# A ring of 16 activation chunks, more weight buffers, and two more pairs with seven products in the gated MLPs of a hybrid decoder

## The chip, the cores and the metric

The kernel runs on one NeuronCore of a Trainium2 chip. The metric is the device time of one execution in microseconds; of several runs the median is given.

## What is computed

The reference is a trunk of two decoder layers, on 256 tokens of width 2048, in float32. Layer 0 mixes by gated linear attention, layer 1 by forgetting attention; both also attend to 256 memory tokens. After each mixer stands the channel mixer, in which the changed work lies (the rotation of the weight parts is written anew for the whole kernel):

```
def conv_ffn(h, w_up, conv_w, conv_b, w_down):
    u = causal_dwconv(h @ w_up, conv_w, conv_b)      # 2048 -> 2 x 5632, width 3 along the tokens
    a, val = split_cols(u, [FFN_HIDDEN, FFN_HIDDEN])
    return (jax.nn.silu(a) * val) @ w_down           # 5632 -> 2048

h = rmsnorm(x, norm_ffn[i])
x = x + conv_ffn(h, ffn_w_up[i], ffn_conv_w[i], ffn_conv_b[i], ffn_w_down[i])
```

## The kernel before

**Float32 by parts.** Every float32 operand of a matmul is taken as a high part (a copy in the fp32r format) and a low part (the rest). A product is three matmuls: high by high, low by high, high by low. ScalarE makes the high part of a weight (`casts`, L242, for pairs L391), VectorE the low part (`lows`, L243, L392).

**Units.** The weights lie in memory in units of 128 x 1024 (512 KB). A unit is loaded by SyncE's queue into a raw slot, split, and multiplied. In the feed-forward (`pair_steps`) a unit has a contraction of 128, two blocks of 128 tokens and two blocks of 512 columns, so 2 x 2 products, 12 matmuls. Raw slots are five pieces of one tile, `home`; `raw_slot` takes the oldest. While a feed-forward runs, two more (`guests`, in the tile `raw2`) join at its first pair with sevens and leave at its end. High and low parts rotate through five tiles each (`whi`, `wlo`), everywhere in the kernel.

**Pairs with sevens.** Two units in a row can be done as a 2 x 2 block product with seven products instead of eight (21 matmuls instead of 24), if sums of the two units' activations and sums of the weights are at hand. The weights' sums are four VectorE additions in place (L448 to L451). The activations' sums are made once: for the up projection by `input_sums` (chunks 6 and, for the panels in `MORE_IN`, 11), for the down projection by `token_sums` when the chunk is made (`SEVEN_DOWN`: chunks 4, 10, 20, 34). After the last such pair of a panel, `early` reads four of its eight banks and adds them up (eight VectorE operations in the down projection); after the last unit, `late` reads the other four.

**Order of the feed-forward.** The hidden width is 44 chunks of 128. `up 0`, `up 4`, ... stand here for the projections of four chunks each (`up_pair(j)`: 16 units for both halves of the gate). The down projection goes in three panels, chunks 0 to 15, 16 to 27 and 28 to 43 (`PARTS`). After up 16 follows down panel 0, with the column blocks 0 and 1 (f=0) and then 2 and 3 (f=2), 16 units each; after up 28 down panel 1, 12 units each; after up 40 the last panel. In the panels 0 and 1, f=0 has no pairs with sevens, f=2 has those of chunks 4 and 10, or 20.

**The convolution.** A panel of four chunks leaves its projection as tokens by channels. It is turned by VectorE (`yu`, L1478) and by a round trip through DRAM on GpSimd's queue: one transfer out (`far`, L661) and four back (`fvt` or `yzu`, L666), for each half of a panel. Then come, for each half, 12 taps on ScalarE (L1428, into three tiles `taps`), two additions of 1024 columns on VectorE (L1435), a SiLU (L1441), the product (L1448, into the tile `cv`) and the split into the ring `m` (L539, L540), with the token sums of the chunks that need them. These steps are put into the program by ticks: each unit is a tick, which adds a credit (1.45, or 1.7 in panels with two pairs; none in a pair), and a step is issued when its due tick has come and credit is left. The return is issued three ticks after the panel's end, the taps come due seven or eight ticks after it. So the convolution of a panel runs beside the units of the next: that of panel 16 beside down panel 0, that of panel 28 beside down panel 1.

**The ring.** The result of the convolution, chunk c, lies in `m[c % 20]`: 16 tiles of a buffer and four more, in layer 0 in the place of the second layer's memory keys and values, which are parked in DRAM meanwhile (`more`), in layer 1 in tiles of its own.

The engines' order of instructions is worked out by a scheduler at build time, from priorities and simulated times; splits and loads have a priority ahead (`AHEAD`), and `issue_after` keeps an instruction behind another on its engine.

Of the kernel before, what the change touches and what calls it, by code (L numbers as in the profile page):

```python
# [30 lines left out]
TAU = 16.0  # L31
BIG = 1e30
PARTS = ((0, 16), (16, 28), (28, 44))
RING = 20
SEVEN_UP = (6,)
SEVEN_DOWN = {4: 0, 10: 1, 20: 0, 34: 1}
SEVEN_MORE = 11
MORE_IN = (1, 2, 5, 6, 7, 8, 9, 10)
SCRATCH = 4096
RAWS = 5  # L40


LEVELS = (64, 16, 4)
# [105 lines left out]
def _trunk(ctx: ExitStack, tc: tile.TileContext, xt, xtok, memt, wp, wgu, gns, gfin, cnv, par, msk, out):  # L149
# [38 lines left out]
    home = rear.tile([P, RAWS * NUNIT], F32, name="raw")  # L188
    slots, coming = [home[:, i * NUNIT : (i + 1) * NUNIT] for i in range(RAWS)], []

    def raw_slot():

        slots.append(slots.pop(0))
        return slots[-1]
    scratch = [sm]
    parked = []

# [5 lines left out]
    def split_apart(unit, spare):  # L203

        off, kcs, n = unit
        w = len(kcs) * n
        with tc.high_priority(offset=AHEAD):
            raw = raw_slot()
            loads.append(nc.sync.dma_start(raw[:, :w], wp[off : off + P * w].rearrange("(p n) -> p n", p=P)))
            hi, lo = [], []  # L210
            for j in range(len(kcs)):
                s = slice(j * n, (j + 1) * n)
                hi.append(spare())
                lo.append(spare())
                casts.append(S.activation(hi[j], raw[:, s], AF.Copy))
                lows.append(V.tensor_tensor(lo[j], raw[:, s], hi[j].bitcast(F32), ALU.subtract))
        return hi, lo

    def split_unit(unit, pieces=1, before=None, between=int):

        off, kcs, n = unit
        w = len(kcs) * n
        with tc.high_priority(offset=AHEAD):
            raw = raw_slot()
            hi = wpool.tile([P, NUNIT], F32R, name="whi", tag="whi", bufs=5)
            lo = wpool.tile([P, NUNIT], F32R, name="wlo", tag="wlo", bufs=5)
            src = wp[off : off + P * w].rearrange("(p n) -> p n", p=P)
            for i in range(pieces):
                s = slice(i * w // pieces, (i + 1) * w // pieces)
                if i:  # L230
                    between()
                loads.append(nc.sync.dma_start(raw[:, s], src[:, s]))
            if n % P:
                a, b, c = (t.rearrange("p (j m) -> p j m", j=len(kcs))[:, :, :n] for t in (raw[:, :w], hi, lo))
                casts.append(S.activation(b, a, AF.Copy))
                lows.append(V.tensor_tensor(c, a, b.bitcast(F32), ALU.subtract))
                return hi, lo
            for i in range(pieces):
                s = slice(i * w // pieces, (i + 1) * w // pieces)
                if before is not None:  # L240
                    before(i)
                casts.append(S.activation(hi[:, s], raw[:, s], AF.Copy))  # L242
                lows.append(V.tensor_tensor(lo[:, s], raw[:, s], hi[:, s].bitcast(F32), ALU.subtract))  # L243
        return hi, lo
# [141 lines left out]
    def split_more(src, n):  # L386

        with tc.high_priority(offset=AHEAD):
            hi = wpool.tile([P, NUNIT], F32R, name="whi", tag="whi", bufs=5)
            lo = wpool.tile([P, NUNIT], F32R, name="wlo", tag="wlo", bufs=5)  # L390
            casts.append(S.activation(hi[:, :n], src, AF.Copy))  # L391
            lows.append(V.tensor_tensor(lo[:, :n], src, hi[:, :n].bitcast(F32), ALU.subtract))  # L392
        return hi, lo

    def pair_steps(units, src, sums, flip, pool, early, late, ahead=0):
# [38 lines left out]
        for k in plan:  # L434
            if k in sums:
                with tc.high_priority(offset=AHEAD):
                    slots[:0] = coming
                    del coming[:]
                    ra, rb = raw_slot(), raw_slot()
                    with tc.issue_after(loads[-1].ins):  # L440
                        for t, (off, _, w) in ((ra, units[k]), (rb, units[k + 1])):
                            loads.append(nc.sync.dma_start(t, wp[off : off + P * w].rearrange("(p n) -> p n", p=P)))
# [39 lines left out]

    def token_sums(r, dst):

        t = r.rearrange("p s (b n) -> p (s b) n", b=2)
        a11, a21, a12, a22 = (t[:, n, :] for n in range(4))
        V.tensor_tensor(a22, a21, a22, ALU.add)
        V.tensor_tensor(a21, a11, a21, ALU.subtract)
        V.tensor_tensor(a11, a22, a11, ALU.subtract)
        V.tensor_tensor(a12, a12, a11, ALU.subtract)  # L490
        halves([dst[:, part] for part in range(2)], t)

    def run(step, hooks={}, count=8):

# [202 lines left out]
    def halves(dst, src):  # L697
        S.activation(dst[0], src, AF.Copy)
        V.tensor_tensor(dst[1], src, dst[0].bitcast(F32), ALU.subtract)
# [705 lines left out]
    def ffn(l, nx, h, m, ys, zs, landing, then, pool, temps, last=None, spare=None):  # L1405
        with tc.tile_pool(name=f"ffn{l}", bufs=1) as fp:
            def held(name, i):
                return pool.tile([P, 2, 4, P], F32R, name=name, tag=f"{name}{i}")

            up_sums = {k: held("usum", k) for k in (*SEVEN_UP, SEVEN_MORE)}  # L1410
            rooms = {i: held("dsum", i) for i in range(2)}
            guest = pool.tile([P, 2 * NUNIT], F32, name="raw2")
            guests = [guest[:, i * NUNIT : (i + 1) * NUNIT] for i in range(2)]
            coming.extend(guests)
            cw = fp.tile([P, 4 * 88], F32, name="cw")
            nc.sync.dma_start(cw, cnv[l])
            taps = [fp.tile([P, 2, 2, T + i], F32, name=f"tap{i}") for i in range(3)]
# [24 lines left out]

            def gated(j, s):

                if s == 0:
                    product[0] = fp.tile([P, 2, T], F32, name="cv", tag="cv")
                    with tc.issue_after(lows[-1].ins):
                        V.tensor_tensor(product[0], taps[0][:, :, 0, :], taps[0][:, :, 1, :], ALU.mult)  # L1448
# [8 lines left out]
            product = [None]  # L1457

            def input_sums(k):

                r = fp.tile([P, 2, T], F32, name="cv", tag="cv")
                for s in range(2):
                    V.tensor_tensor(r[:, s, :], h[k + s][:, 0, :].bitcast(F32), h[k + s][:, 1, :].bitcast(F32), ALU.add)
                token_sums(r, up_sums[k])
# [141 lines left out]
            slots[:] = [s for s in slots if not any(s is g for g in guests)]  # L1606

    def preparing(name, dst, pool, far, kept=None, tag="blk", queue=nc.sync):

# [43 lines left out]
    with tc.tile_pool(name="stash", bufs=1) as st:  # L1653
# [4 lines left out]
        with tc.tile_pool(name="turn1", bufs=1) as tp:  # L1658
# [23 lines left out]
    with tc.tile_pool(name="store", bufs=1) as op:  # L1682
# [131 lines left out]
```

## Time and profile before

| | us |
|---|---|
| runs | 2209.04, 2209.77, 2210.29 |
| median | 2209.77 |
| profiled execution, its own time | 2210.43 |
| its span, first to last instruction | 2208.6 |
| TensorE busy | 2195.5 (99%) |
| VectorE busy | 1828.1 (83%) |
| ScalarE busy | 1435.6 (65%) |
| GpSimd busy | 136.8 (6%) |
| feed-forward of layer 0, about | 457 to 1106 |
| feed-forward of layer 1, about | 1494 to the end |

The busy time of an engine counts its instructions without waiting. The ends of matmuls are modelled: a matmul of 512 columns is drawn longer (0.39 us) than its distance to the next, so starts say more than busy time does. A row of windows gives for a stretch its length and then each engine's busy time and number of instructions. In a row of the timeline, "[0.23 <-ACT whi L391]" is the idle time of the engine before the instruction and what ended it. PE is TensorE's matmul, PEld its weight load, DVE VectorE, ACT ScalarE, POOL GpSimd, SP SyncE.

### The profile page before, as it was taken

The numbers are of one execution on the slowest core, as the hardware profiler recorded it, in microseconds if no ns is written. First come the engines' busy times: TensorE is split into PE (matmuls) and PEld (weight loads), VectorE is DVE, ScalarE is ACT, GpSimd is POOL, SyncE is SP. The second block draws the span as 40 slices with busy tenths as digits, with TensorE's granted clock in tenths as the row PEclk, the third lists the DMA queues.
The fourth block names the chain that finished last, engine by engine and source line by source line (L and its number), as shares of the span: only waits on it lengthen the run. The fifth ranks groups of instructions, "written<-read, shape, count | busy, mean of one in ns | idle before, by whom it ended". The sixth has DMA issues, their size and how long they took to land.

```text
span 2208.6 us, 30197 instructions
## 1 busy us (share of the span) xinstructions
PE 2195.5 (99%) x10285; PEld 1845.1 (84%) x10285; DVE 1828.1 (83%) x2715; ACT 1435.6 (65%) x2280; POOL 136.8 (6%) x257
## 2 busy tenths in 40 slices
PE   9999999999999999999999999999999999999998
PEld 7888888888888888888888998888888888888886
DVE  7768976689998889889987669668898888988996
ACT  6655655557787468657865555555888657765874
POOL 0000000001100000001010000000100000100000
PEclk9999999999999999999999999999999999999999
DMA  9767667776777567666877767776777667776783
GB/s 371 249 223 220 194 211 228 250 237 227 245 254 253 185 226 252 221 223 222 269 244 248 227 201 245 225 242 228 233 261 230 232 200 246 244 235 210 232 282 112
DMA packets 166291, 515.41 MB, mean 233 GB/s; under 512 B 20780, under 2 KB 42552, under 8 KB 166136
## 3 DMA queue, kind: packets, MB, share of 16 engines
q1 hardware_dynamic: 149064, 460.99, 63.4%
q0 software_dynamic: 16496, 51.71, 7.4%
q8 instruction: 80, 1.31, 0.2%
q10 hardware_dynamic: 576, 0.79, 0.1%
q14 instruction: 75, 0.61, 0.1%
HBM read 469.62 MB, written 43.79 MB: 232 GB/s over the span
## 4 chain that ended last, share of the span: by engine, by line
PE 95%; DVE 2%; DMA 1%; ACT 1%; issue 0%; SPq 0%; DVEq 0%; ACTq 0%
PE acc L421 27%; PE acc L347 26%; PE ps_s L421 15%; PE ps_o L421 7%; PE ps_t L421 7%; PE acc L318 3%; PE acc L273 3%; PE ps_s L347 2%; PE acc L377 2%; PE acc L271 1%; ACT whi L391 0%; DMA raw<-wp 0%; DMA far<-blk 0%; DVE wlo L392 0%; PE ps_s L1046 0%
## 5 line engine op out<-in xcount | busy, mean ns | idle before, releaser
L243 DVE TENSOR_TENSOR wlo<-raw,whi 128x1024 fp32r<-128x1024 f32 (+2 forms) x685 | 815.3, 1205 | 211.7 <-ACT whi L242 194.6
L242 ACT ACTIVATE whi<-raw 128x1024 fp32r<-128x1024 f32 (+2 forms) x685 | 703.1, 1045 | 339.7 <-PE acc L347 137.7
L391 ACT ACTIVATE whi<-raw 128x1024 fp32r<-128x1024 f32 (+1 forms) x184 | 173.8, 954 | 180.6 <-DVE raw L449 67.8
L347 PE MATMUL acc<-whi,B 128*128 128x512 f32 (+3 forms) x1248 | 290.8, 369 | 0.0
L347 PEld LDWEIGHTS acc<-whi,B 128*128 128x128 f32 x1248 | 226.8, 188 | 28.1
L392 DVE TENSOR_TENSOR wlo<-raw,whi 128x1024 fp32r<-128x1024 f32 (+1 forms) x184 | 199.2, 1088 | 35.7 <-ACT whi L391 30.6
L421 PE MATMUL acc<-whi,mix 128*128 128x512 f32 x746 | 191.3, 389 | 0.0
L421 PE MATMUL acc<-whi,B 128*128 128x512 f32 x720 | 187.4, 389 | 0.0
L421 PEld LDWEIGHTS acc<-whi,mix 128*128 128x128 f32 x746 | 140.0, 188 | 29.2
L347 PE MATMUL acc<-wlo,B 128*128 128x512 f32 (+3 forms) x624 | 159.1, 369 | 0.0
L421 PEld LDWEIGHTS acc<-whi,B 128*128 128x128 f32 x720 | 135.1, 188 | 28.3
L347 PEld LDWEIGHTS acc<-wlo,B 128*128 128x128 f32 x624 | 114.2, 188 | 14.6
L1428 ACT ACTIVATE tap<-fvt,cw 128x256 f32<-128x256 f32 x264 | 120.4, 535 | 5.1 <-DMA fvt<-far 5.1
L1428 ACT ACTIVATE tap<-yzu,cw 128x256 f32<-128x256 f32 x264 | 120.3, 533 | 4.3 <-DMA yzu<-far 3.5
L1435 DVE TENSOR_TENSOR tap<-tap,tap 128x1024 f32<-128x1024 f32 x88 | 107.1, 1217 | 14.2 <-ACT tap L1428 13.9
L421 PE MATMUL acc<-wlo,mix 128*128 128x512 f32 x373 | 105.2, 389 | 0.0
L421 PE MATMUL acc<-wlo,B 128*128 128x512 f32 x360 | 104.0, 389 | 0.0
L421 PE MATMUL ps_s<-whi,mix 128*128 128x512 f32 x374 | 103.8, 389 | 0.0
L421 PE MATMUL ps_s<-whi,B 128*128 128x512 f32 x324 | 89.9, 389 | 0.0
L421 PEld LDWEIGHTS ps_s<-whi,mix 128*128 128x128 f32 x374 | 70.2, 188 | 14.6
L421 PEld LDWEIGHTS acc<-wlo,mix 128*128 128x128 f32 x373 | 70.0, 188 | 14.5
L421 PEld LDWEIGHTS acc<-wlo,B 128*128 128x128 f32 x360 | 67.6, 188 | 14.0
(503 smaller groups left out, 3921.4 us busy)
## 6 DMA issues: line engine op xcount, KB each, us to landing
raw<-wp SPq DMA_DIRECT2D x741, 512.0 KB, 4.6
fvt<-far POOLq DMA_DIRECT2D x100, 128.0 KB, 4.8
raw<-wp SPq DMA_DIRECT2D x32, 384.0 KB, 3.5
far<-yu POOLq DMA_DIRECT2D x22, 512.0 KB, 3.1
far<-yzu POOLq DMA_DIRECT2D x22, 512.0 KB, 3.2
yzu<-far POOLq DMA_DIRECT2D x88, 128.0 KB, 4.6
raw<-wp SPq DMA_DIRECT2D x24, 388.0 KB, 3.6
x<-xtok SPq DMA_DIRECT2D x8, 512.0 KB, 7.2
```

Source lines behind the costliest of these rows:

```text
L242: casts.append(S.activation(hi[:, s], raw[:, s], AF.Copy))
L243: lows.append(V.tensor_tensor(lo[:, s], raw[:, s], hi[:, s].bitcast(F32), ALU.subtract))
L271: mm = TE.matmul(acc[p][c][:, :T], w[:, s], both[:, 0, :], start=False, stop=end and j == 3)
L273: mm = TE.matmul(acc[p][c], w[:, s], both, start=u == j == 0, stop=end and j == 3)
L318: mm = TE.matmul(acc[b][:, :n], src[kcs[j] - base][:, part, b * P : (b + 1) * P], w, start=u == 0 and low == part == j == 0, stop=u == end ...
L347: mm = TE.matmul(acc[b][:, :n], src[kc - base][:, part, b * P : (b + 1) * P], ready[low][:, j * room : j * room + n], start=i == low == pa ...
L377: mm = TE.matmul(acc[b][:, :n], src[kc - base][:, part, b * P : (b + 1) * P], w, start=i == low == part == j == 0, stop=i == end and low = ...
L391: casts.append(S.activation(hi[:, :n], src, AF.Copy))
L392: lows.append(V.tensor_tensor(lo[:, :n], src, hi[:, :n].bitcast(F32), ALU.subtract))
L421: r = TE.matmul(bank[name], x, w, start=name not in begun, stop=last)
L1428: S.activation(by_run(taps[i][:, s, c, i:]), zs[slot][:, :, 2 * c + s], AF.Copy if i else AF.Identity, bias=0.0 if i else w[3], scale=w[2 ...
L1435: V.tensor_tensor(taps[0], taps[0], taps[n][:, :, :, :T], ALU.add)
```

## The change

- The ring has 16 tiles, those of the buffer. So chunk 16 goes to the tile of chunk 0, which down panel 0 reads.
- The convolution of panel 16 comes due 30 ticks after the panel instead of 8, that of panel 28 after 22 ticks (`PUT_OFF`).
- The two places of 128 x 1024 that the ring gives up become a sixth high and a sixth low part, for the length of a feed-forward. High, low and raw now rotate by one class, `Ring`, over slices of one tile each.
- A third raw guest, so eight raw slots in the feed-forward.
- f=0 of down panel 0 takes chunk 10, and of panel 1 chunk 20, as a pair with sevens (`ONCE`).
- The product is made in place in `taps[0]`; `cv` is gone. `input_sums` works in `temps(3)`, the fourth temporary of `early`, in the pool `turn1` or `store`.
- `SCRATCH`, the build's `dynamic_dma_scratch_size`, is 2048 instead of 4096.

```
-RING = 20
+RING = 16
-SCRATCH = 4096
-RAWS = 5
+SCRATCH = 2048
+SLOTS = 5
+RAW_GUESTS = 3
+PUT_OFF = {16: 30, 28: 22}
+ONCE = {0: 10, 1: 20}
...
+    class Ring:
+        def __init__(self, home):
+            self.slots, self.coming = [home[:, i * NUNIT : (i + 1) * NUNIT] for i in range(SLOTS)], []
+        def take(self):
+            self.slots.append(self.slots.pop(0))
+            return self.slots[-1]
+        def join(self):
+            self.slots[:0] = self.coming
+            del self.coming[:]
+        def leave(self, guests):
+            self.slots[:] = [s for s in self.slots if not any(s is g for g in guests)]
+
+    raws = Ring(rear.tile([P, SLOTS * NUNIT], F32, name="raw"))
+    his, los = [Ring(wpool.tile([P, SLOTS * NUNIT], F32R, name=name, tag=name, bufs=1)) for name in ("whi", "wlo")]
...
-            raw = raw_slot()
-            hi = wpool.tile([P, NUNIT], F32R, name="whi", tag="whi", bufs=5)
-            lo = wpool.tile([P, NUNIT], F32R, name="wlo", tag="wlo", bufs=5)
+            raw = raws.take()
+            hi, lo = his.take(), los.take()
...
-                    slots[:0] = coming
-                    del coming[:]
-                    ra, rb = raw_slot(), raw_slot()
+                    for ring in (raws, his, los):
+                        ring.join()
+                    ra, rb = raws.take(), raws.take()
...
-            guest = pool.tile([P, 2 * NUNIT], F32, name="raw2")
-            guests = [guest[:, i * NUNIT : (i + 1) * NUNIT] for i in range(2)]
-            coming.extend(guests)
+            guest = pool.tile([P, RAW_GUESTS * NUNIT], F32, name="raw2")
+            guests = [guest[:, i * NUNIT : (i + 1) * NUNIT] for i in range(RAW_GUESTS)]
+            for ring, lent in ((raws, guests), (his, more[:1]), (los, more[1:])):
+                ring.coming.extend(lent)
...
+                r = taps[0][:, :, 0, :]
                 if s == 0:
-                    product[0] = fp.tile([P, 2, T], F32, name="cv", tag="cv")
                     with tc.issue_after(lows[-1].ins):
-                        V.tensor_tensor(product[0], taps[0][:, :, 0, :], taps[0][:, :, 1, :], ALU.mult)
-                r = product[0]
+                        V.tensor_tensor(r, r, taps[0][:, :, 1, :], ALU.mult)
...
             def input_sums(k):
-                r = fp.tile([P, 2, T], F32, name="cv", tag="cv")
+                r = temps(3).rearrange("p (s t) -> p s t", s=2)
...
-                turns = [turn(j + 2 * h_, 7 if not h_ and j // 4 + 1 in MORE_IN else 8) for h_ in range(2)]
+                turns = [turn(j + 2 * h_, PUT_OFF.get(j) or (7 if not h_ and j // 4 + 1 in MORE_IN else 8)) for h_ in range(2)]
...
-                    drive(down_pair(l, p, f, src, {c - lo: t for c, t in sums.items() if f}, count[2] % 2, pool,
+                    drive(down_pair(l, p, f, src, {c - lo: t for c, t in sums.items() if f or c == ONCE[p]}, count[2] % 2, pool,
                                     lambda: (temps(0), temps(1))))
...
-                more.append(const.tile([P, 2, 2, T], F32R, name="more" + tag, tag=tag))
-            ffn(0, n, bufB, bufA + [t[:, i] for t in more for i in range(2)], ys, turned3, ys, then, tp, temps)
+                more.append(const.tile([P, NUNIT], F32R, name="more" + tag, tag=tag))
+            ffn(0, n, bufB, bufA, more, ys, turned3, ys, then, tp, temps)
...
-        more = [op.tile([P, 2, T], F32R, name=f"more{i}") for i in range(RING - KC)]
-        ffn(1, n, bufA, bufB + more, ys, zs, zs, then, op, temps, last, spare)
+        more = [op.tile([P, NUNIT], F32R, name=f"more{i}") for i in range(2)]
+        ffn(1, n, bufA, bufB, more, ys, zs, zs, then, op, temps, last, spare)
```

More of the change, by code (lines that the diff above doesn't have):

```diff
@@ L187, in _trunk @@
     loads, casts, lows, ends, last_mm, sent = [], [], [], [], [], []
[L188 to L194, printed above, removed]
+    class Ring:
[11 more added lines that the diff above has]
+    his, los = [Ring(wpool.tile([P, SLOTS * NUNIT], F32R, name=name, tag=name, bufs=1)) for name in ("whi", "wlo")]
     scratch = [sm]
@@ L223, in split_unit @@
         with tc.high_priority(offset=AHEAD):
-            raw = raw_slot()
-            hi = wpool.tile([P, NUNIT], F32R, name="whi", tag="whi", bufs=5)
-            lo = wpool.tile([P, NUNIT], F32R, name="wlo", tag="wlo", bufs=5)
+            raw = raws.take()
+            hi, lo = his.take(), los.take()
             src = wp[off : off + P * w].rearrange("(p n) -> p n", p=P)
@@ L388, in split_more @@
         with tc.high_priority(offset=AHEAD):
-            hi = wpool.tile([P, NUNIT], F32R, name="whi", tag="whi", bufs=5)
-            lo = wpool.tile([P, NUNIT], F32R, name="wlo", tag="wlo", bufs=5)
+            hi, lo = his.take(), los.take()
             casts.append(S.activation(hi[:, :n], src, AF.Copy))
@@ L483, in token_sums @@
     def token_sums(r, dst):
-        t = r.rearrange("p s (b n) -> p (s b) n", b=2)
-        a11, a21, a12, a22 = (t[:, n, :] for n in range(4))
+        t = r.rearrange("p s (b n) -> p s b n", b=2)
+        a11, a21, a12, a22 = (t[:, s, b] for s in range(2) for b in range(2))
         V.tensor_tensor(a22, a21, a22, ALU.add)
@@ L490, in token_sums @@
         V.tensor_tensor(a12, a12, a11, ALU.subtract)
-        halves([dst[:, part] for part in range(2)], t)
+        halves([dst[:, part].rearrange("p (s b) n -> p s b n", s=2) for part in range(2)], t)
     def run(step, hooks={}, count=8):
@@ L1403, in add_out, with ffn @@
                 proj_tm((*key, f), src, last if f == 3 and last is not None else evac_of(f), spare if f == 3 else None)
-    def ffn(l, nx, h, m, ys, zs, landing, then, pool, temps, last=None, spare=None):
+    def ffn(l, nx, h, m, more, ys, zs, landing, then, pool, temps, last=None, spare=None):
         with tc.tile_pool(name=f"ffn{l}", bufs=1) as fp:
@@ L1455, in gated @@
                         token_sums(r, sums[j])
-            product = [None]
             def input_sums(k):
-                r = fp.tile([P, 2, T], F32, name="cv", tag="cv")
+                r = temps(3).rearrange("p (s t) -> p s t", s=2)
                 for s in range(2):
@@ L1605, in ffn @@
                         hooks.get((f, u), int)()
-            slots[:] = [s for s in slots if not any(s is g for g in guests)]
+            for ring, lent in ((raws, guests), (his, more[:1]), (los, more[1:])):
+                ring.leave(lent)
     def preparing(name, dst, pool, far, kept=None, tag="blk", queue=nc.sync):
```

## The prediction

> **What bounds the kernel now.** I read the page's busy times first, then the chain that ended last, then who TensorE waited for, and then the feed-forward stages one by one.
>
> ```profile
> span 2208.6 us, 30197 instructions
> PE 2195.5 (99%) x10285; PEld 1845.1 (84%) x10285; DVE 1828.1 (83%) x2715; ACT 1435.6 (65%) x2280; POOL 136.8 (6%) x257
> PE 95%; DVE 2%; DMA 1%; ACT 1%; issue 0%; SPq 0%; DVEq 0%; ACTq 0%
> ...
> 883.82 32.64 PE acc L421 x144
> ...
> PE ps_t L421 <- ACT whi L391: 2.0, 4, 1.2
> ```
>
> TensorE is busy for 99% of the span and carries 95% of the chain. The chain row gives its beat: 144 matmuls of 512 columns in 32.64 us, 0.2267 us per matmul with no hole. The last row lists most of what it waited for in the feed-forward pairs: 2.0 us for ScalarE's high part of a summed weight (L391). So the time is a count of matmuls times 0.2267 us, plus small stalls, as long as ScalarE and VectorE prepare weights faster than one unit per 12 matmuls, 2.72 us.
>
> ```profile
> core 0: us, PE busy (x) PEld busy (x) DVE busy (x) ACT busy (x) POOL busy (x), PEclk, DMA share, GB/s
> ...
> 501.10:543.30 42.20, 42.20 (x188) 34.95 (x187) 37.80 (x44) 32.93 (x51) 5.45 (x10) 1.00 0.71 233
> 543.30:585.50 42.20, 41.90 (x184) 33.91 (x183) 39.51 (x49) 32.73 (x52) 5.46 (x10) 1.00 0.71 236
> ...
> 671.20:714.70 43.50, 43.50 (x194) 36.02 (x193) 36.67 (x42) 31.52 (x52) 5.47 (x10) 1.00 0.78 255
> 714.70:756.80 42.10, 42.10 (x187) 34.88 (x186) 36.20 (x44) 21.38 (x23) 0.00 (x0) 1.00 0.60 199
> 756.80:799.10 42.30, 42.30 (x188) 35.02 (x187) 33.06 (x37) 23.08 (x26) 0.00 (x0) 1.00 0.60 201
> ...
> 841.20:883.80 42.60, 42.54 (x188) 34.92 (x187) 42.17 (x55) 34.30 (x57) 5.51 (x10) 1.00 0.75 241
> ...
> 1986.00:2028.20 42.20, 42.20 (x188) 34.95 (x187) 33.44 (x37) 22.98 (x26) 0.00 (x0) 1.00 0.63 207
> ...
> 457.00:1106.00 649.00, 648.35 (x2855) 535.10 (x2854) 575.69 (x713) 453.01 (x678) 60.32 (x110) 1.00 0.71 235
> 1494.00:2143.00 649.00, 647.42 (x2851) 534.36 (x2850) 575.25 (x712) 454.48 (x679) 60.40 (x110) 1.00 0.71 236
> ```
>
> These are, of the first layer, up 4, up 8, the first two column blocks of down panel 0 (f=0), its other two (f=2), up 20 and up 28, and up 32 of the second; the last two rows are all of each layer's feed-forward. TensorE idles 0.65 + 1.58 = 2.23 us in 1298 us. Its clock is 1.00 throughout. VectorE is the second engine: 42.17 of 42.60 us in up 28 and 39.51 in up 8, the stages where a convolution meets two pairs with sevens; up 20 and up 32 have two pairs too, but no convolution, and VectorE has 9 us free.
>
> **The pairs (SEVEN and ONCE).** A unit costs 12 matmuls, so a plain pair 24; a pair with sevens costs 7 products of 3, 21. The change makes one pair of f=0 in down panel 0 (chunk 10) and one in down panel 1 (chunk 20) such a pair, in both layers: 4 x 3 = 12 matmuls fewer, 12 x 0.2267 = 2.72 us, all on the path. The Trainium skill ("TensorE: Matmul & The Clock Gate", Back-to-back issue gap) puts a warm 512-column matmul at 215.7 ns start to start; by it the sum would be 2.59 us, and the trace's rows read 5% more. The row decides.
>
> What a pair adds elsewhere is read from these rows.
>
> ```profile
> L243 DVE TENSOR_TENSOR wlo<-raw,whi 128x1024 fp32r<-128x1024 f32 x196 | 235.4, 1221 | 37.5 <-ACT whi L242 35.6
> L392 DVE TENSOR_TENSOR wlo<-raw,whi 128x512 fp32r<-128x512 f32 x23 | 15.9, 689 | 11.3 <-ACT whi L391 8.7 <-PE acc L421 2.5
> L448 DVE TENSOR_TENSOR raw<-raw 128x512 f32<-128x512 f32 x23 | 15.9, 690 | 0.3
> L1435 DVE TENSOR_TENSOR tap<-tap,tap 128x1024 f32<-128x1024 f32 x41 | 49.9, 1216 | 8.9 <-ACT tap L1428 8.7
> L1448 DVE TENSOR_TENSOR cv<-tap 128x512 f32<-128x512 f32 x20 | 13.7, 685 | 0.0
> L540 DVE TENSOR_TENSOR mix<-cv,mix 128x256 fp32r<-128x256 f32 x24 | 9.2, 421 | 0.0
> L1428 ACT ACTIVATE tap<-fvt,cw 128x256 f32<-128x256 f32 x252 | 114.8, 535 | 5.1 <-DMA fvt<-far 5.1
> ```
>
> VectorE splits 0.69 + 3 x 1.22 us and forms four sums of 0.69, 7.1 us against 2 x 1.22; f=0 now also runs the early read-out, eight operations of 0.69 (5.5 us, the size of the sums' row). Together +10.2 us per pair, beside TensorE. In down panel 0 f=0 VectorE had 36.67 of 43.50 us. The convolution of panel 16 leaves it: four adds of 1.22, two products of 0.69, four splits of 0.42 are 7.9 us; nearly all of them lay there. So about 36.7 - 7 + 10.2 = 39.9 of 42.8 us. Hidden; if the cover fails, one pair costs what a pair in up 8 costs (0.51 us, below). The raw loads, two of 512 KB, stay two. ScalarE's casts grow by 1.5 units a pair, in a stage where it had 31.5 of 43.5 us.
>
> **The ring of 16 and the put-off.** Panels 16 to 19 now write over m[0..3], which down panel 0 still reads, so their convolution comes due 30 ticks after their projection instead of 8, three ticks before up 20 begins. Of the 48 taps, adds and splits of both halves a few taps stay ahead of up 20, the rest falls into up 20: VectorE 33.06 + 7.9 = 41.0 of 42.2 us, ScalarE 23.08 + 24 taps of 0.535 + some 3 = 39 at most. The same for panel 28 and up 32: 33.44 + 7.9 = 41.3. Both stand below up 28's 42.17, which stalls little. The POOL queue's two round trips (far, four returns) are issued when they were; only the readers are later, so the slot of the return stays taken longer, until the middle of up 20; the next returns are not due before its end. Cost from both sides: no stall, or the worst that such a stage shows now:
>
> ```profile
> 555.24 1.07 PE L421 MATMUL ps_s<-whi,usum 128*128 128x512 f32 x4
> 556.38 0.74 PE L421 MATMUL ps_t<-whi,usum 128*128 128x512 f32 x2
> ...
> 568.80 0.85 PE L421 MATMUL ps_s<-whi,usum 128*128 128x512 f32 x3
> 569.88 0.74 PE L421 MATMUL ps_t<-whi,usum 128*128 128x512 f32 x2 [0.23 <-ACT whi L391]
> ...
> 559.08 4.29 ACT L1428 ACTIVATE tap<-fvt,cw 128x256 f32<-128x256 f32 x10
> 563.26 0.63 ACT L391 ACTIVATE whi<-raw 128x512 fp32r<-128x512 f32 x1
> ...
> 567.32 1.06 ACT L391 ACTIVATE whi<-raw 128x1024 fp32r<-128x1024 f32 x1 [1.98 <-DVE raw L449]
> 568.77 1.06 ACT L391 ACTIVATE whi<-raw 128x1024 fp32r<-128x1024 f32 x1 [0.39 <-PE acc L421]
> ```
>
> Three matmuls from 568.80 on the beat end at 569.48; the next starts at 569.88 and the one after it 0.34 later: 0.40 + 0.11 = 0.51 us, of which the profile shows 0.23 as idle. Up 8's other pair, four matmuls from 555.24 and the next at 556.38 instead of 556.15, loses 0.23 + 0.11 by the same reckoning, so a bad stage costs 0.85. Four stages: 0 to 3.4 us; I take 0.3 each, nearer to up 28, which shows 0.06 of idle at one place, than to up 8: 1.2 us.
>
> **Sixth high and low part.** In those rows ten taps stand ahead of the pair's first cast, and its last cast waits for a part that TensorE still holds. One more part lets the casts be queued one unit, 2.72 us, sooner, five times the stall. Eleven places in both layers stall, 2.23 us of shown idle plus about 0.28 each that the modelled ends hide: 5.3 us. The first pair of each layer is another matter (next part, 2.0 us), and one at the end of layer 1 is not a pair (0.6). So 0 to 2.7 us can be gained here; I take 1.2, and it cancels the put-off. In layer 0 the two guests lie where mk1 and mv1 were parked at the very start, so they are free at once.
>
> **Eighth raw slot.**
>
> ```profile
> raw<-wp SPq DMA_DIRECT2D x741, 512.0 KB, 4.6
> ...
> fvt<-far POOLq DMA_DIRECT2D x100, 128.0 KB, 4.8
> ```
>
> A load lands in 4.6 us, and seven slots already hold seven units of 2.72 us; the eighth gains nothing, and loads that start sooner only wait longer: 0.
>
> **First pair of a layer.**
>
> ```profile
> 1498.01 5.31 DMA far<-blk
> ...
> 1503.71 5.30 DMA raw<-wp
> ...
> 1503.41 0.63 ACT L698 ACTIVATE usum<-cv 128x512 fp32r<-128x512 f32 x1 [1.45 <-DMA far<-blk]
> 1504.80 0.43 DVE L1463 TENSOR_TENSOR cv<-mix 128x256 f32<-128x256 f32 x1
> L488 DVE TENSOR_TENSOR cv<-cv 128x128 f32<-128x128 f32 x5 | 1.5, 296 | 0.0
> ...
> 1514.07 0.73 PE L421 MATMUL ps_t<-whi,usum 128*128 128x512 f32 x2 [1.18 <-ACT whi L391]
> ```
>
> The guests' loads start when far<-blk has landed, land 5.30 us later, and the fourth cast comes late: 1.18 us shown. Three guests in one tile wait the same way, so this stays. What moves: the input sums of unit 6 now use temps(3), in the pool whose usum waits for that landing too (the third row). Two adds of 0.43, four sums of 0.30, ScalarE's half 0.63 and VectorE's, 0.69 like the sums above, make 3.4 us after 1503.3: 1506.7, while the pair's loads land at 1509. Nothing, up to 3.4 us per layer if they are queued badly. The sums of unit 11 have to wait until panel 0's fourth temp is read, so 2.7 us of VectorE move to up 4 (37.80 to 40.5): 0, at most another 0.9. The product in place frees cv, and taps[0] must wait for two splits (0.8 us) more; eight taps of the other two tiles (3.4 us and more) come first: 0.
>
> **SCRATCH at half.** It is the memory that the build sets aside for POOL's transfers. No row shows how much of it they use; the nearest is this.
>
> ```profile
> 603.00 2.18 POOL L666 DMA_DIRECT2D fvt<-far  x4 [4.44 <-ACT whi L391]
> ```
>
> A burst of four takes 0.55 us each, without a pause, once ScalarE has freed the slot. I take 0. From below nothing is gained; from above see the last rival.
>
> **Sum.** -2.72 + 1.2 - 1.2 = -2.7 us. The profiled execution took 2210.43 us, its span 2208.6; it stands 0.66 above the median 2209.77. Span 2205.9, profiled time 2207.7, median 2207.0. A measurement tells 0.2% (4.4 us) from no change at best, so this is "no change" by that measure.
>
> **Rivals.** A, the sixth part clears the stalls and the put-off adds none: -2.72 - 2.7 = -5.4, 2204.4. For it: ten taps ahead of a cast. Against: in up 28 the lack is VectorE time, not parts. B, up 20 and up 32 stall as up 8 does and nothing clears: -2.72 + 3.4 = +0.7, 2210.5; the change then gives back what it saves. For it: 41.0 of 42.2 us. C, VectorE becomes the bound of up 20 and up 32: its idle in those stages (9 us) is waiting for casts and cannot all be used; if 5 us cannot, it needs 46 us of 42.2, 3.8 us lost in each of four stages: -2.7 + 15.2, 2222. It decides from 1.8 us per stage. Against: up 28 fills 42.17 of 42.60. D, POOL's transfers are held up. The Trainium skill ("SBUF — State Buffer", Summary: rules for kernel authors) says GpSimd's descriptor writing starves while VectorE has the shared port in its fast modes; the rows show bursts of 2.18 us beside a full VectorE, so it does not show today. As a mechanism here: if each return waited for the landing of the one before, a burst would take 4 x 4.8 = 19 us and a panel's two end 34 us late; 6 us are spare (four ticks of 2.72 less a landing) and six prepared units give 16, so some 12 us per panel and, over 22 panels, 2470.
>
> **How the numbers follow.** Forecast (2205.4 to 2209) 0.58, A (2203.5 to 2205.4) 0.12, B (2209 to 2211.5) 0.20, C 0.08, D 0.02. Predicted 2207.0. The range takes the forecast and about three quarters of A and of B, 0.82 in all: 2204.0 to 2211.0; C and D stay out. Faster by over 0.2% (under 2205.35) is A, 0.12; slower is C and D, 0.10; the rest, 0.78, is within.
>
> **What would show it.** Right: f=0 of down panel 0 42.8 us long (43.5 now) and of panel 1 32.0 (32.6), three matmuls fewer each; no convolution before the last units of f=2; up 20 with VectorE near 41 us and TensorE idle under 0.3; up 8 with less than its 0.30 idle. Wrong: a first pair waiting longer than 1.18 us, TensorE waiting for L391 in up 20 or up 32 by more than 1 us each, a POOL burst longer than 2.2 us, or holes in the other layers' stages, where five parts stay five.

## The result and the profile after

The changed kernel takes 2223.58 us (median of four runs, 2220.95 to 2225.07); the kernel before, beside it on the same chip, 2209.40 (2209.04 to 2210.29). The ratio is 1.0062, 95% interval 1.0045 to 1.0080: slower by 14 us, where 2207.0 was forecast and 2211.0 was the end of the range. The page of the profiled execution (its own time 2225.07):

```profile
span 2223.3 us, 30061 instructions
PE 2198.0 (99%) x10273; PEld 1840.9 (83%) x10273; DVE 1853.4 (83%) x2771; ACT 1440.0 (65%) x2292; POOL 136.7 (6%) x257
PE 92%; DVE 3%; ACT 2%; DMA 2%; issue 1%; POOL 0%; DVEq 0%; ACTq 0%; POOLq 0%
```

TensorE has 12 matmuls fewer, as counted in the forecast, and is still 14.7 us later at the end. VectorE is at 83% as before. GpSimd's 136.7 us are the 136.8 of before, with half the scratch memory. The chain has lost 3% to VectorE, ScalarE and DMA. Whom TensorE waited for (us in total, times, longest):

```profile
PE ps_t L434 <- ACT whi L404: 3.9, 2, 2.0
PE acc L434 <- ACT whi L404: 3.4, 5, 1.7
PE acc L434 <- DVE wlo L257: 2.3, 4, 1.4
PE acc L434 <- ACT whi L256: 1.8, 3, 0.7
```

L404 and L256 are the casts of the pairs and of the single units (L391 and L242 before), L257 the single units' low part. Waits for a cast are longer, and waits for low parts and for single units are new in the feed-forward. By stages of layer 0, in windows (length, busy time of each engine, clock):

```profile
core 0: us, PE busy (x) PEld busy (x) DVE busy (x) ACT busy (x) POOL busy (x), PEclk, DMA share, GB/s
669.65:712.50 42.85, 42.85 (x191) 35.48 (x190) 37.45 (x48) 20.91 (x25) 5.47 (x10) 1.00 0.74 247
...
754.65:799.40 44.75, 42.79 (x187) 34.67 (x186) 37.00 (x46) 27.37 (x40) 0.00 (x0) 1.00 0.52 180
799.40:843.60 44.20, 42.84 (x188) 34.71 (x187) 38.90 (x46) 31.54 (x48) 5.52 (x10) 1.00 0.75 241
843.60:885.75 42.15, 42.15 (x187) 34.90 (x186) 40.26 (x54) 30.47 (x45) 5.49 (x10) 1.00 0.73 257
949.70:1083.00 133.30, 128.71 (x559) 103.91 (x558) 118.95 (x146) 91.07 (x135) 10.96 (x20) 1.00 0.67 228
```

These are down panel 0 f=0, up 20, up 24, up 28, and up 32 to up 40 together. The first is what the pair promised, 42.85 us without a hole. Up 20 idles 1.96 us and up 24 1.36; up 24 has no convolution of the put-off kind. VectorE has 37.00 of 44.75 us in up 20: it is not full. Up 28, the fullest stage before, has no hole. Up 32 to up 40 idle 4.6 us; none of these three lost over 0.3 us before.

A count of the same kind for every kernel of this document: of the distances between two matmul starts, whatever goes beyond 0.2267 us (of those over 0.24), added up over both layers' feed-forward. It is taken from one profiled execution of each kernel; that of "the change, in order" was the slowest of its 11 runs, 3.6 us above their median. The column of casts is explained below, the kernels under the experiments.

| us | casts out of order | first pairs (up 0) | up 8 | up 12, 16 | up 20, 24 | down panel 1 | up 28 to 40 | all, with the rest |
|---|---|---|---|---|---|---|---|---|
| before | 4 | 2.0 | 1.8 | 0 | 0 | 0 | 1.2 | 6.1 |
| the change | 119 | 0.2 | 0.5 | 0 | 7.5 | 0 | 11.7 | 22.9 |
| pairs alone | 4 | 0.9 | 1.7 | 0 | 0 | 1.9 | 1.2 | 7.0 |
| put-off alone | 4 | 2.8 | 1.7 | 0 | 0 | 0 | 0 | 6.3 |
| the change, no pairs | 103 | 1.2 | 1.3 | 0 | 5.9 | 0 | 7.8 | 16.2 |
| the change, cv back | 135 | 0 | 0.4 | 10.0 | 5.0 | 6.8 | 25.0 | 49.5 |
| fixed slices alone | 84 | 0 | 7.2 | 7.5 | 0 | 1.8 | 2.9 | 23.6 |
| the change, free tiles | 5 | 1.9 | 3.0 | 0 | 0 | 0.4 | 0 | 7.2 |
| pairs and put-off | 4 | 1.2 | 1.7 | 0 | 0 | 1.4 | 0 | 6.1 |
| product in place alone | 4 | 3.7 | 3.0 | 0 | 0 | 0 | 0 | 8.5 |
| fixed slices, in order | 6 | 3.5 | 0.1 | 0 | 0 | 0 | 0 | 5.4 |
| the change, in order | 7 | 5.7 | 2.3 | 0 | 0 | 0 | 0 | 11.8 |
| the change, cv back, in order | 5 | 1.2 | 0.7 | 0 | 0 | 3.1 | 3.7 | 8.6 |
| pairs and put-off, fixed slices, in order | 6 | 2.1 | 0.1 | 0 | 0 | 1.4 | 2.2 | 7.6 |

22.9 - 6.1 - 2.72 for the matmuls saved = 14.1 of the span's 14.7 us: the time lies in the feed-forwards, in holes of TensorE.

What such a hole looks like, in up 20 (timeline; ScalarE, VectorE, TensorE one after the other):

```profile
769.75 1.57 ACT L404 ACTIVATE whi<-raw 128x512 fp32r<-128x512 f32 x2
771.22 1.05 ACT L404 ACTIVATE moremk<-raw 128x1024 fp32r<-128x1024 f32 x1
779.30 1.06 ACT L256 ACTIVATE whi<-raw 128x1024 fp32r<-128x1024 f32 x1 [7.02 <-PE ps_s L434]
780.27 1.04 ACT L256 ACTIVATE moremk<-raw 128x1024 fp32r<-128x1024 f32 x1
781.21 1.04 ACT L404 ACTIVATE whi<-raw 128x1024 fp32r<-128x1024 f32 x1
782.16 1.05 ACT L256 ACTIVATE whi<-raw 128x1024 fp32r<-128x1024 f32 x1
...
777.12 0.69 DVE L463 TENSOR_TENSOR raw<-raw 128x512 f32<-128x512 f32 x1
780.39 1.23 DVE L257 TENSOR_TENSOR wlo<-raw,whi 128x1024 fp32r<-128x1024 f32 x1 [2.58 <-ACT whi L256]
781.54 0.68 DVE L464 TENSOR_TENSOR raw<-raw 128x512 f32<-128x512 f32 x1
...
779.36 0.62 PE L434 MATMUL ps_s<-whi,B 128*128 128x512 f32 x2
780.26 0.39 PE L434 MATMUL ps_s<-moremv,usum 128*128 128x512 f32 x1
782.31 1.20 PE L434 MATMUL acc<-whi,usum 128*128 128x512 f32 x4 [1.65 <-ACT whi L404]
```

Which unit a row belongs to comes from matching the built program with the trace, instruction by instruction. The casts at 779.30 and 780.27 are those of units 13 and 14 of the panel. The one at 781.21 is a cast of the pair 11 and 12, which the program has two units earlier, and TensorE waits for it from 780.5 to 782.31. Its sum of weights (L463) was there at 777.8. But ScalarE runs its instructions in their order (in the trace they come line by line as in the built list): unit 13's cast stands ahead of it and waited 7.02 us for matmuls into the bank ps_s; unit 14's follows, 1.9 us for both. Unit 13's slice is, in the built program, the one in which the pair's own first high part lay, so its cast had to wait until the pair's matmuls had read that part. Units 9 and 10, which the program also has ahead of 13, are cast only after that (782.16 and later). On VectorE the same: the pair's last sum (L464) stands behind unit 13's low part, which waited 2.58 us. A cast or low part of a later unit thus holds up an earlier one.

This inversion can be counted in the built programs, on ScalarE's list of some 910 weight casts: before, 4 stand behind one that the program has later; after, 119. The table's column has this count for every kernel: the four kernels with 84 to 135 have holes of 16 to 50 us, the ten with 4 to 7 have 5.4 to 11.8.

### The profile page after: what moved, and what is told of

The parts are those of the page before. It is cut to its first block, busy times and chain, and to the rows that moved or that the text cites. A ratio compares the mean times of both kernels' runs of the same rounds, so it can differ in the third digit from the quotient of the medians.

```text
span 2223.3 us, 30061 instructions
## 1 busy us (share of the span) xinstructions
PE 2198.0 (99%) x10273; PEld 1840.9 (83%) x10273; DVE 1853.4 (83%) x2771; ACT 1440.0 (65%) x2292; POOL 136.7 (6%) x257
## 4 chain that ended last, share of the span: by engine, by line
PE 92%; DVE 3%; ACT 2%; DMA 2%; issue 1%; POOL 0%; DVEq 0%; ACTq 0%; POOLq 0%
PE acc L361 26%; PE acc L434 26%; PE ps_s L434 14%; PE ps_o L434 7%; PE ps_t L434 6%; PE acc L332 3%; PE acc L287 3%; PE ps_s L361 2%; PE acc L391 2%; PE acc L285 1%; DMA raw<-wp 1%; ACT whi L256 1%; DVE wlo L257 1%; DVE wlo L405 1%; ACT tap L1442 1%
## 5 line engine op out<-in xcount | busy, mean ns | idle before, releaser
L257 DVE TENSOR_TENSOR wlo<-raw,whi 128x1024 fp32r<-128x1024 f32 (+2 forms) x610 | 725.6, 1198 | 198.3 <-ACT whi L256 181.0
L256 ACT ACTIVATE whi<-raw 128x1024 fp32r<-128x1024 f32 (+2 forms) x610 | 629.6, 1043 | 402.9 <-PE acc L361 141.6
L361 PEld LDWEIGHTS acc<-whi,B 128*128 128x128 f32 x1248 | 226.8, 188 | 28.1
L405 DVE TENSOR_TENSOR wlo<-raw,whi 128x1024 fp32r<-128x1024 f32 (+1 forms) x164 | 176.5, 1084 | 35.9 <-ACT whi L404 22.9
L404 ACT ACTIVATE whi<-raw 128x1024 fp32r<-128x1024 f32 (+1 forms) x164 | 154.6, 949 | 75.8 <-PE acc L434 20.4
L434 PE MATMUL acc<-whi,B 128*128 128x512 f32 x654 | 175.2, 390 | 1.4 <-ACT whi L256 1.4
L434 PE MATMUL acc<-whi,mix 128*128 128x512 f32 x620 | 163.9, 390 | 0.3 <-ACT whi L256 0.3
L434 PEld LDWEIGHTS acc<-whi,B 128*128 128x128 f32 x654 | 122.4, 188 | 28.4 <-ACT whi L256 2.9
L434 PEld LDWEIGHTS acc<-whi,mix 128*128 128x128 f32 x620 | 116.0, 188 | 26.0 <-ACT whi L256 2.0
L361 PEld LDWEIGHTS acc<-wlo,B 128*128 128x128 f32 x624 | 114.2, 188 | 14.7
L434 PE MATMUL acc<-wlo,mix 128*128 128x512 f32 x310 | 92.8, 390 | 1.5 <-DVE wlo L257 1.5
L434 PE MATMUL ps_s<-whi,B 128*128 128x512 f32 x278 | 80.6, 389 | 0.0
L361 PE MATMUL acc<-whi,mix 128*128 128x512 f32 x280 | 70.2, 390 | 0.0
```

Source lines behind the costliest of these rows:

```text
L361: mm = TE.matmul(acc[b][:, :n], src[kc - base][:, part, b * P : (b + 1) * P], ready[low][:, j * room : j * room + n], start=i == low == pa ...
L434: r = TE.matmul(bank[name], x, w, start=name not in begun, stop=last)
```

## The experiments

The theories. P: the put-off brings too much work into up 20 and up 32 (rival C of the prediction, whose 2222 us lay near the result). Q: the new pairs overload their stages. R: the product in place and the input sums in temps(3) delay the convolution. S: the change to fixed slices, handed out by `Ring` in the program's order, in place of pool tiles for high and low parts, lets the scheduler put casts of later units ahead of earlier ones.

**The first four: the pairs alone, the put-off alone, the change without the pairs, the change with cv.**

```
# e1, on the kernel before
-    ... if f}
+    ... if f or c == {0: 10, 1: 20}[p]}
# e2, on the kernel before
+    {16: 30, 28: 22}.get(j) or (7 if ... else 8)
# e3, on the change
-    ... if f or c == ONCE[p]}
+    ... if f}
# e4, on the change: the product and the input sums in the tile cv again; its place is that of one raw guest
+    product[0] = fp.tile([P, 2, T], F32, name="cv", tag="cv")
-RAW_GUESTS = 3
+RAW_GUESTS = 2
```

> The kernel before with the two new pairs (f=0 takes chunk 10, and chunk 20) and nothing else. Theory P (the put-off convolution loads VectorE at the start of up 20 and up 32, and the pairs are innocent): 12 matmuls fewer, 2.7 us faster, 2206.0 to 2207.5. Rival Q (the new pairs overload VectorE beside down panels 0 and 1): slower than 2211, with TensorE waiting in down panel 0 f=0 or up 20. Rival R (the product in place) says nothing against 2206.7.

> The kernel before with the convolutions of panels 16 and 28 due 30 and 22 ticks after their projection, the ring still 20, five high and low parts, product in its own tile. Theory P: up 20, up 24, up 32, up 36 and up 40 stall as in the changed kernel or more, since there are only five parts: +15 to +25 us, 2224 to 2235. Rivals Q and R: within 3 us of 2209.4.

> The changed kernel without the two new pairs. Theory P: 12 matmuls more and the same stalls, +2.7 us, 2225 to 2228. Rival Q: the stalls of up 20 to up 40 go, 2208 to 2211. Rival R: as P.

> The changed kernel with the product and the input sums in a tile of their own again (cv), paid for by the third raw guest. Theory P: 2221 to 2226, nothing changes. Rival R (the taps of the next half wait for the splits and token sums that now read taps[0], and ScalarE's casts stand behind them): most of the 17 us of stalls go, 2207 to 2213.

Measured, beside 2209.61 for the kernel before: pairs alone 2209.94 (ratio 1.0002, 0.9993 to 1.0012), put-off alone 2209.58 (1.0002, 0.9993 to 1.0011), the change without the pairs 2220.61 (1.0050, 1.0034 to 1.0067), the change with cv 2252.87 (1.0195, 1.0180 to 1.0210). Up 20 with the put-off alone, in a window:

```profile
757.10:799.20 42.10, 42.10 (x187) 34.89 (x186) 40.39 (x50) 28.31 (x40) 0.00 (x0) 1.00 0.62 205
```

VectorE works 40.39 of 42.10 us there, more densely than in the changed kernel's up 20, and TensorE has no hole. P is out. The pairs alone change nothing that shows: they save 2.7 us of matmuls and lose 1.9 in down panel 1. Without them the change stays slow, 3.0 us faster than with them although it does 12 matmuls more: Q is out as the main cause. And undoing what R blames makes the change 29 us slower still, with holes in stages that had none (up 12, up 28, down panel 1); this run also gives up the third raw guest, so R by itself is tried below. For three of the four no theory's range held the result: the pairs alone came between P (2207.5 at most) and Q (above 2211), the change without them between Q (2211 at most) and P (2225 at least), the change with cv far above all. What goes wrong moves from stage to stage with each edit, which points away from the amount of work in a stage and to the order of instructions.

**The second four: fixed slices alone, the change with free tiles, pairs with put-off, the product in place alone.**

```
# e5, on the kernel before: five slices of one tile, handed out in turn
-hi = wpool.tile([P, NUNIT], F32R, name="whi", tag="whi", bufs=5)
-lo = wpool.tile([P, NUNIT], F32R, name="wlo", tag="wlo", bufs=5)
+hi, lo = part_slot(0), part_slot(1)
# e6, on the change: the reverse, with five tiles, so without the sixth part
-his, los = [Ring(wpool.tile([P, SLOTS * NUNIT], ...)) for name in ("whi", "wlo")]
+his, los = Free("whi"), Free("wlo")    # take() is wpool.tile([P, NUNIT], ..., bufs=SLOTS)
# e7, on the kernel before: the edits of e1 and e2
# e8, on the kernel before: the product and the input sums as the change has them
+    V.tensor_tensor(r, r, taps[0][:, :, 1, :], ALU.mult)
+    r = temps(3).rearrange("p (s t) -> p s t", s=2)
```

> The kernel before, where the five high and the five low parts are no longer five free tiles but fixed slices of one tile, handed out in the order of the program, as the class Ring does; nothing else. Theory S (the cause is the fixed hand-out: a cast waits for its own slice while another is free, so the scheduler lets later units' casts pass it, and VectorE and TensorE follow): TensorE stalls appear in the up stages that have two pairs, +5 to +15 us, 2214 to 2225. Its program has 84 of 905 casts behind a cast of a later piece, against 4 before. Rival R (the product in place and the input sums in temps(3)): 2209 to 2210.5, no change.

> The changed kernel with five free tiles each for the high and low parts, as before, so without the sixth; ring of 16, put-off, pairs, product in place and eight raw slots stay. Theory S: 5 casts out of order, the stalls go, 2206 to 2209. Rival R: 2218 to 2226. A third possibility, that put-off and pairs only hurt together: above 2212.

> The kernel before with the two new pairs and the put-off and nothing else (ring 20, five free parts, seven raw slots). Each alone was no change; the pairs alone lost 1.9 us of their 2.7 in down panel 1 f=0, where the convolution of panel 28 stood. Theory S: the put-off takes it away from there, so the 2.7 us come through, 2206 to 2208. If put-off and pairs hurt together: above 2211.

> The kernel before with the product in place in taps[0] and the input sums in temps(3). Theory S: 2208.5 to 2210.5. Rival R: the stalls of the changed kernel, above 2214.

Measured, beside 2209.45: fixed slices alone 2226.70 (1.0075, 1.0061 to 1.0089); the change with free tiles 2208.92 (0.9997, 0.9988 to 1.0006); pairs and put-off 2207.58 (0.9993, 0.9984 to 1.0002); in place alone 2211.77 (1.0010, 1.0000 to 1.0019).

An edit that adds no work, and changes only which memory a high or low part is given, costs 17 us, more than the whole change; taking it back out of the change, and the sixth part with it, gives 14.7 us back. Whom TensorE waited for with fixed slices alone (L396 and L248 are the casts of pairs and of single units), and up 20 and up 24 of the change with free tiles in a window, which has no hole:

```profile
PE ps_s L426 <- ACT whi L396: 5.9, 3, 2.8
PE acc L426 <- ACT whi L248: 3.3, 2, 2.3
PE acc L426 <- ACT whi L396: 2.4, 3, 1.2
```

```profile
757.00:841.30 84.30, 84.30 (x373) 69.82 (x372) 79.19 (x97) 60.87 (x90) 5.51 (x10) 1.00 0.72 235
```

The casts out of order are 84 with fixed slices alone and 5 in the change with free tiles. S holds so far, though 2226.70 is above the 2225 at which its range ended, and most of the holes of e5 lie in up 8 and up 16, elsewhere than the change's. The product in place came out between S (2210.5 at most) and R (above 2214): R is out as the main cause, but the edit isn't free.

What the other two show. With pairs and put-off, the first column blocks of down panel 1 lose 0.7 us in each layer (TensorE's timeline):

```profile
895.97 1.07 PE L421 MATMUL ps_s<-whi,dsum 128*128 128x512 f32 x4
897.48 0.74 PE L421 MATMUL ps_t<-whi,dsum 128*128 128x512 f32 x2 [0.44 <-ACT whi L391]
```

Four matmuls on the beat end at 896.88; the next starts at 897.48: 0.60, and 0.11 for the first one's longer distance. With the product in place, up 8 loses 0.6 us more in each layer, as it also does in the change with free tiles (3.0 in the table for 1.8). The rest of what is lost stands at the first pair of layer 1, 3.1 us in place of 1.5:

```profile
1510.83 0.72 PE L421 MATMUL acc<-whi,mix 128*128 128x512 f32 x2 [0.46 <-ACT whi L391]
1512.90 1.19 PE L421 MATMUL ps_s<-whi,usum 128*128 128x512 f32 x4 [0.87 <-ACT whi L391]
1515.49 0.73 PE L421 MATMUL ps_t<-whi,usum 128*128 128x512 f32 x2 [0.94 <-ACT whi L391]
```

That second part need not be the edit's. The pair's loads (L442) are issued when the transfer far<-blk has landed, which took 7.0 us in this execution and 5.31 in that of the kernel before. So long SyncE's queue waited with them (us in total, times, longest):

```profile
SPq L442 <- DMA far<-blk: 6.7, 1, 6.7
```

The landing is 1.7 us longer, the loss 1.6 us. With the put-off alone, which leaves the input sums as they were, it took 6.12 us and the first pair lost 2.1; in the change with free tiles, which has the input sums in temps(3), 5.07 and 1.2.

**The third three: the order itself.** If S is right, keeping each cast and each low part behind the one before it must give the time back while the slices stay fixed.

```
# e9, on e5; e10, on the change; e11, on e4
-casts.append(S.activation(hi[:, s], raw[:, s], AF.Copy))
+with tc.issue_after(casts[-1].ins):
+    casts.append(S.activation(hi[:, s], raw[:, s], AF.Copy))
... (the low parts in the same way, behind lows[-1])
```

> The kernel before with the five fixed slices of e5_fixed_slots_only, but each cast told to stay behind the cast before it in the program on ScalarE, and each low part behind the low part before it on VectorE. If the changed order is the cause (theory S as refined), 6 casts out of order instead of 84 and no stalls beyond those of before: 2208 to 2211. If fixed slices cost by themselves (a cast must wait for one certain slice): above 2215.

> The changed kernel, all of it, with the casts and the low parts kept in the order of the program. If the order is the cause: the stalls of up 20 to up 40 go; 12 matmuls fewer, the sixth part clears up 8 and the first pair, the product in place costs its 2.3 us: 2205 to 2209. If not: above 2215.

> As e10_after_ordered, but product and input sums in a tile of their own again and two raw guests instead of three. If the order is the cause and the product in place costs 2.3 us: 2203 to 2207, the fastest of all. If the order isn't: as e4_after_cv, above 2240.

Measured, beside 2209.67: fixed slices in order 2208.76 (0.9998, 0.9989 to 1.0008); the change in order 2209.52 (1.0000, 0.9991 to 1.0009); the change with cv, in order, 2210.03 (1.0003, 0.9994 to 1.0012). So the order alone takes 17.9, 14.1 and 42.8 us off the same three kernels, and brings all three to within 1 us of the kernel before. Casts out of order are now 6, 7 and 5. Fixed slices as such cost nothing that shows. Casts and low parts were tied together, so their shares aren't known, and why the scheduler turns them round when the slices are fixed was not looked into. What TensorE still waits for in the pairs of e9 and of e10 (L399 and L407 are their casts):

```profile
PE ps_t L430 <- ACT whi L399: 1.3, 2, 0.9
```

```profile
PE ps_t L438 <- ACT whi L407: 3.5, 4, 0.9
PE acc L438 <- ACT whi L407: 1.6, 2, 1.1
```

That the change with cv in order would come to 2203 to 2207 was a miss: it loses 3.7 us in up 28 to up 40 and 3.1 in down panel 1, at the pairs. The ordered change ended just above its range (2209). In the execution that was profiled, its slowest, it loses 5.7 us at the first pairs, 4.6 of it in layer 1, where far<-blk took 7.01 us again. That the tie of the casts adds to this isn't shown: the other two kernels with tie and pairs lose 1.2 and 2.1 there.

**The last: what is good, in one kernel.** The kernel before with pairs, put-off, five fixed slices, in order.

```
# e12, on e9: the edits of e1 and e2
```

> The kernel before with the two pairs, the put-off, five fixed slices for high and low parts, and every cast and low part kept behind the one before it; the ring of 20, cv, two raw guests and five parts stay. If only the inverted order made the change slow, and the edits add up, this is the kernel of pairs and put-off (profiled span 2206.6) less the stalls of up 8 that the ordered order cleared (0.85 + 0.87, to 0.00 + 0.08), plus what the ordered order added at the first pair of layer 1 (2.89 instead of 1.45): between 2205.5 and 2208.5, median 2207. If fixed slices cost something of their own even in order, or if the ordered order and the pairs stand in each other's way (as the stalls of 1.3 to 1.7 us in up 28, down panel 1 and up 40 of the ordered change with cv suggest), 2209.5 to 2211, and the sixth part is not what made that one slow.

Measured: 2210.19 (2208.89 to 2213.39) beside 2209.35, ratio 1.0004, 0.9995 to 1.0013. A miss for the sum of gains, as the second case of the expectation had it: up 8 is clear (0.0 and 0.1) as in e9, but up 40 loses 1.1 in each layer, where neither part alone lost anything. With the ring of 16 and a sixth part besides (e11, 2210.03) the time is the same, so these gain nothing that shows here. Pairs and put-off in free tiles, 2207.58, remain the fastest kernel, 0.07% below the one before, with an interval that still holds 1.

A sixth high and low part with free tiles was not tried: six such tiles do not fit into the memory that is left. Neither the eighth raw slot nor the smaller scratch memory was tried by itself; both are in the change with free tiles, which loses nothing to the kernel before.

## Why the prediction was wrong

**The step that failed** is the sum itself: -2.72 + 1.2 - 1.2 has no term for the hand-out of high and low parts. The prediction counts the sixth part and speaks of "five parts stay five", and passes over the line of the change by which all of them become slices of one tile taken in turn. No instruction is added by it, and no row of the profile before has a price for it. It measured +17.2 us alone and +14.7 within the change (there with the sixth part), and what it does is shown by the built order: casts and low parts of later units stand ahead of earlier ones, and TensorE waits for those. With the order held, the same slices cost nothing that shows. The bound was wrong too: what the prediction lists as costs from above are stalls in a stage by its work, and an order of instructions made anew isn't bounded by any stage's work. One of its signs of being wrong did come: TensorE waits 1.65 us at once for a pair's cast in up 20. Since the order differs all through the changed kernel, the other terms can't be read off it; they are read off the experiments.

**The pairs.** The count was right: 10273 matmuls for 10285, 42.85 us in down panel 0 f=0 (42.8 foretold). "Hidden" was right there. In panel 1 it holds in the changed kernel (no hole), but not in pairs and put-off, where each layer gives back 0.7 us, near the 0.51 named for a failed cover. Pairs and put-off together came to -1.9 us by the medians, which the interval doesn't tell from nothing; the same two terms of the sum, -2.72 + 1.2, say -1.5.

**The put-off.** Taken at +1.2, measured at 0: up 20 and up 32 have no hole, in e2 and e7. The load was foretold well, VectorE at 40.39 of 42.10 us in e2's up 20 for 41.0 of 42.2; that such a stage stalls was not.

**The sixth part.** The changed kernel has 0.5 us of stalls left in up 8 and 0.2 at the first pairs, which looks like rival A. But fixed slices of five, in order, clear up 8 as well (1.8 to 0.1), and the change in order has 2.3 us there. It is the order of casts that decides there; a gain from the part itself wasn't seen.

**The product in place** was taken at 0 because other taps come first. With the input sums in temps(3) it measured +2.3 us alone (the interval begins at 1.0000). Of this 1.3 us lie in up 8, in both layers together; the 1.6 us at the first pair of layer 1 go with a longer landing of far<-blk, as said. So the prediction's "nothing, up to 3.4 us per layer" for the input sums stays open, and which of the two moves costs the time in up 8 wasn't separated.

**The rivals.** C forecast 2222 and the kernel took 2223.6, but that is luck: it asked for a VectorE without time in up 20, and that engine has 7.75 us free there (44.75 - 37.00) and waits 2.58 us for ScalarE in the hole shown. The put-off alone has VectorE fuller in up 20, and no hole there. Holes in up 24, up 36 and up 40, which get no put-off convolution, speak against C too. B's stalls did not come with the put-off alone either. D did not happen: GpSimd's busy time is the same to 0.1 us.

## What to carry to other kernels

When a scheduler works out the engines' order at build time, an edit that only renames or regroups buffers is a change of order, and has to be priced as such: compare the built order of the instructions that feed the bound engine before reading any stage of the profile. Where engines run in order and several producers share one, tie those that must stay in the consumer's order explicitly; here two such ties per split were worth 14 to 43 us in the three kernels that lacked the order. And a forecast that hits the time by the wrong mechanism is found out by the stage table: ask where the holes are, not only how long they are. Last, compare a single place of two profiles only after the transfers ahead of it took the same time.

## What the runs showed of the hardware

A long stall can cost more than its length. With fixed slices alone, in up 8 (TensorE's timeline, then windows with the granted clock in the third column from the end):

```profile
566.69 1.07 PE L426 MATMUL ps_s<-whi,usum 128*128 128x512 f32 x4
570.09 1.90 PE L426 MATMUL acc<-whi,B 128*128 128x512 f32 x6 [2.33 <-ACT whi L248]
571.79 1.05 PE L426 MATMUL ps_s<-wlo,usum 128*128 128x512 f32 x2
572.64 1.05 PE L426 MATMUL ps_t<-whi,usum 128*128 128x512 f32 x2
```

```profile
567.50:570.10 2.60, 0.27 (x3) 0.01 (x1) 0.98 (x1) 2.07 (x3) 0.00 (x0) 1.00 0.61 202
571.30:574.80 3.50, 3.50 (x10) 2.70 (x10) 3.50 (x4) 3.50 (x7) 0.00 (x0) 0.51 0.86 257
574.80:580.00 5.20, 5.20 (x24) 4.29 (x23) 3.26 (x5) 4.12 (x10) 0.00 (x0) 1.00 0.89 303
```

After 2.33 us of idle TensorE restarts at full speed, and 1.3 us later eight matmuls come at 0.427 us instead of 0.2267, with the clock at 0.51: 8 x 0.2 = 1.6 us on top of 2.5 us of stall. The Trainium skill ("TensorE: Matmul & The Clock Gate", What's actually happening) describes a clock that falls to half after an idle window of some 3.4 us, on a window that runs freely; the half clock agrees with the trace. The window itself is shown by no run here. The Trainium skill's advice to avoid idle gaps beyond some 3 us ("Why this matters for your kernels") draws the line too far out: 2.33 us sufficed here. Length alone doesn't decide: in the same kernel's up 16 a distance of 3.15 us between two starts was followed by no half clock. In the change with cv, six such stretches add up to 8.6 us; the changed kernel, whose longest distance between two starts is 2.41 us, has none in its feed-forwards.

Besides, at full clock the first matmul after a stall takes 0.11 us longer to the next start (0.335 to 0.341 us instead of 0.2267), so ten short stalls cost 1.1 us more than their own length.
